# Layer 0 of a two-layer encoder: modulation steps from the last input piece on, short-conv taps beside the output projection, one more quarter in split products

## The chip, the cores and the metric

The kernel runs on one core of one Trainium2 chip. The metric is device time in microseconds (us) of the whole program; the time before is the median of three runs, 2281.75 us (2279.96 to 2282.76). Smaller is better.

## The reference

Two layers, each on 256 positions of 2048 channels in float32. Cut to what matters here (written with `*` for elementwise products):

```
mod = silu(c) @ w_mod[l] + b_mod[l]            # six vectors of 2048
shift_m, scale_m, gate_m, shift_f, scale_f, gate_f = split(mod)
h = layer_norm(x) * (1 + scale_m) + shift_m
proj = h @ w_in[l]                             # 2048 x 4288
uv, q_c, kv_c, k_r, sb, sc, sh, ag = split(proj)
y_a = gmlp(uv)                                 # group A: uses U and V columns
y_b = latent_attention(q_c, kv_c, k_r)         # group B
y_c = sb * causal_conv3(sc * sh)               # group C: E (=sb), C (=sc, sh)
y_d = silu(layer_norm(causal_conv31(a * sigmoid(g))))   # group D, a and g from ag
y = concat(y_a, y_b, y_c, y_d) @ w_out[l]      # 2048 x 2048
x = layer_norm(ALPHA * x + (1 + gate_m) * y)
h = layer_norm(x) * (1 + scale_f) + shift_f
y = (silu(causal_conv3(gate)) * val) @ ffn_w_down,  gate, val = split(h @ ffn_w_up)
x = layer_norm(ALPHA * x + (1 + gate_f) * y)
```

Only layer 0 from the end of its input projection to the end of its output projection is touched.

## The kernel before, in words

**Two kinds of product.** A weight is used either exactly (float32, tiles `wexact`, one DMA straight into place, PE takes two passes) or split: the DMA brings `wraw`, ACT rounds it to `whi` (L461), DVE subtracts to get `wlo` (L462), and PE does three products of the rounded kind in their place, `whi` with the rounded data, `wlo` with it, `whi` with the data's rest. The tiles of a raw load come from a pool of four 1 MB buffers (`rawp`), which modulation loads (`wmod`) share; the split and the exact tiles come from `splitp`, four of each of two tags (`weights`, L426). In the output projection `plain` lists the column chunks that use exact weights.

**Modulation.** For a vector of `mod`, DVE multiplies each 128x2048 block of w_mod by one column of silu(c) and adds it into `macc` (`mod_step`, L235 to L240), sixteen steps a vector; a bias row is added for gates (L358). `mod_stream` (L338) yields after each step, with the sums on PE (`ps_gate` for a gate, L289; `ps_mod` for the others) done as chores in between. The order of vectors is GATE_M, SHIFT_F, SCALE_F, GATE_F of layer 0, then layer 1's. `pump` (L376) adds the phase's rate from RATES to a credit and does as many steps as the credit holds; `stream` (L405) calls it once for each unit of work, and issues that unit's weight loads first.

**Order of layer 0.** `by_pieces` (L1299) takes the input's contraction rows in five PIECES as their modulation gets ready; in each piece PE does D's products and between them those of the groups U, V and E (`side`). Then follow group B (`latent_group`, eight units, exact), group C (1024 columns, eight units, exact), and the output projection (`out_proj`, L669) in the column chunks (0, 1024), (1024, 512), (1536, 512): eight units split, four exact, four exact, with a unit of a 512-wide chunk holding four contraction tiles and of the first chunk two. The last chunk's products are done at the end, first tile t = 0, then t = 1, with the norm's work on DVE.

**Background work.** `background` holds small jobs that `stream` takes, `bg` of them per unit; `drain_background` does the rest at once. STEPS gives `bg` by phase: the conformer conv's thirty taps on DVE (`convD`, L920), each with four scalings on ACT (L919) into `scaled`, and `norm_d`. `attend` (L1080) follows group B: it transposes the copied latent rows on PE into `ps_q`, `ps_kv`, and goes on to `kc`, `ps_kr`, `ps_qn`. `mix_c` and `conv_c` (L1247: one ACT scaling and two DVE taps for each of four blocks, `yc`) and `mix_e` (L1261: `yc` times E's sums) are done in one go after C. `out_proj`'s `load_unit` (L795) splits the data too (`act_pair`, `split`).

**Engines.** Each engine takes its instructions in the order in which the program is written down by this Python code, so what is pumped or drained where sets the order on DVE, ACT, PE and the DMA queue of SP. Tiles' buffers come free when their last reader is done.

Of the kernel before, what the change touches and what calls it, by code (L numbers as in the profile page):

```python
# [18 lines left out]
KT = D // P  # L19
# [13 lines left out]


RATES = [
    dict(B=1.6, C=2.2, out=1.5, up=0.7, down=0.7),
    dict(D=1.0, U=0.0, V=0.0, B=0.0, C=0.0, E=0.9, out=0.6, up=0.3, down=0.7),
]

STEPS = [  # L40
    dict(B=1, C=3, up=2),
    dict(U=7, B=4, C=4, E=8, up=2),
]

PIECES = ((0, 2), (2, 2), (4, 4), (8, 4), (12, 4))
# [5 lines left out]
def encoder_kernel(ctx: ExitStack, tc: tile.TileContext, A: dict, consts: bass.AP, out: bass.AP):  # L51
# [321 lines left out]
    def phase(l, name):  # L373
        pace["rate"] = RATES[l][name]
# [26 lines left out]
    def drain_background():  # L401
        while background:
            background.pop(0)()
# [214 lines left out]
    def run(g):  # L618
        units, load, products, end, bg = g
        for u in range(units):  # L620
            stream(lambda: load(u), lambda item, u=u: products(item, u), bg)
            pending.extend(postponed)
            postponed.clear()
        pending.append(end)
# [44 lines left out]
    def out_proj(l, w, src, order, gate_of, name, post_g, post_b, before, then, plain=(), bg=0):  # L669
# [113 lines left out]
        for c0, width in CHUNKS:  # L783
            last = c0 + width == D
            nk = 2048 // width
            units = nkt // nk
            state = {"tail": []}

            def load(u, c0=c0, width=width, nk=nk, units=units, last=last):
                item = load_unit(u, c0, width, nk, units, last)  # L790
                if last and u == units - 1:
                    gains()
                return item

            def load_unit(u, c0, width, nk, units, last):  # L795
                kt = order[nk * u]
                assert order[nk * u : nk * u + nk] == list(range(kt, kt + nk))
                spare = nk if last and units - 4 <= u < units - 2 else 0
                exact = c0 in plain
                parts = weights(w, kt, nk, c0, width, exact, spare)  # L800
                s4 = src[kt // 4]
                if exact:
                    return parts, [(s4[:, kt % 4 + k, :], None) for k in range(nk)]
                acts = []
                for k in range(0, nk, 2):
                    pair = kept.get(kt + k)
                    if pair is None:
                        pair = act_pair("a")
                        split(pair, s4[:, kt % 4 + k : kt % 4 + k + 2, :])
                        if nkt == KT:  # L810
                            kept[kt + k] = pair
                    for j in range(2):
                        acts.append([h[:, j, :] for h in pair[:2]])
                return parts, acts

            def unit(item, u, state=state, c0=c0, width=width, nk=nk, last=last, units=units):
                if u == 0:
                    state["ps"] = [
                        [acc_tile(f"{name}_{c0}{t}{i}") for i in range(width // 512)] for t in range(2)
                    ]  # L820
                if last and u >= units - 4:
                    state["tail"].append((item, u))
                    return
                for t in range(2):
                    products(t, item, state["ps"], u, nk)

            for u in range(units):
                stream(lambda: load(u), lambda item, u=u, unit=unit: unit(item, u), bg, not last)

            def done(state=state, c0=c0, nk=nk, last=last):  # L830
                if c0 == 0:
                    box["gate"] = gate_of()
                for t in range(2):
                    for item, u in state["tail"]:
                        products(t, item, state["ps"], u, nk)
                    if t == 0 and last and before is not None:
                        before()
                for t in range(2):
                    finish(t, state["ps"], c0)
                    if last:  # L840
                        norm(t)
                if last:
                    closed.append(True)

            pending.append(done)


    def mixers(l, w_in, Y, hF=None, between=None):
# [397 lines left out]

        def conv_c(ch):  # L1247
            yc = Y["c"] = slot("yc").rearrange("p (j s) -> p j s", j=4)
            for j in range(4):
                act.activation(out=yc[:, j, :], in_=ch[:, j, :], func=AF.Copy, scale=SW(2, j))  # L1250
                for k in range(2):
                    dve.scalar_tensor_tensor(
                        out=yc[:, j, 2 - k :],
                        in0=ch[:, j, : S - 2 + k],
                        scalar=SW(k, j),
                        in1=yc[:, j, 2 - k :],
                        op0=ALU.mult,
                        op1=ALU.add,
                    )

        def mix_e(cps, _):  # L1261
            yc = Y["c"]
# [36 lines left out]
    def by_pieces(l, w_in, hF, between, mix_d, mix_u, gelu_v, mix_v, mix_b, mix_c, mix_e):  # L1299
# [49 lines left out]
        for q, (k0, nkt) in enumerate(PIECES):  # L1349
            ahead = between(q + 1) if q + 1 < len(PIECES) else ([], None)  # L1350
            exact = k0 < PLAIN_KT
            loaded = {}

            def load(g, kt):

                c0, width = (C_AG, 1024) if g == "D" else (cols[g], 512)
                nk = min(2048 // width, nkt)
                for j, p in enumerate(weights(w_in, kt, nk, c0, width, exact or g != "D")):
                    loaded[(g, kt + j)] = p

            mods_left = list(ahead[0])
            units = len(mods_left)

            def some_mods(share):
                while mods_left and (units - len(mods_left)) < units * share:
                    mods_left.pop(0)()

            def d_part(kt, half):
                if ("D", kt) not in loaded:
                    load("D", kt)  # L1370
                chan_major(accD, kt, loaded[("D", kt)], range(4 * half, 4 * half + 4), kt == 0, kt == KT - 1)

            turns_d = [(kt, h) for kt in range(k0, k0 + nkt) for h in range(2)]
            n = len(turns_d) // 4
            for s in range(4):
                mine = turns_d[s * n : (s + 1) * n]
                if ("D", mine[0][0]) not in loaded:
                    load("D", mine[0][0])
                some_mods((0.3, 0.7, 1.0, 1.0)[s])
                if s == 3 and ahead[1] is not None:  # L1380
                    ahead[1]()
                for kt, h in mine:
                    d_part(kt, h)
                if s < 3:
                    g = "UVE"[s]
                    load(g, k0)
                    some_mods((0.5, 0.85, 1.0)[s])
                    side(g, [(kt, loaded[(g, kt)]) for kt in range(k0, k0 + nkt)], k0, nkt)
        mix_d(accD, None)
        mix_u(sums["U"], None)  # L1390
        for t in range(2):
# [5 lines left out]

        def mix_ce(cps, tps):
            mix_c(cps, tps)
            mix_e(sums["E"], None)  # L1400

        run(group(w_in, C_SC, 1024, f"C{l}", mix_ce, hF=hf, bg=STEPS[l]["C"]))
        drain_background()
# [151 lines left out]
    for l in range(DEPTH):  # L1555
        Y = {}
        if l == 0:
            hF = [slot(f"hF{q}").rearrange("p (j s) -> p j s", j=4) for q in range(4)]
            mixers(l, A["w_in"][l], Y, hF, lambda q: piece(q, hF))
        else:  # L1560
            mixers(l, A["w_in"][l], Y)
        phase(l, "out")
        flush()
        out_proj(
            l,
            A["w_out"][l],
            [Y[n] for n in "abcd"],
            list(range(KT)),
            gate(l, GATE_M),
            f"o{l}",  # L1570
            A["post_mix_g"][l],
            A["post_mix_b"][l],
            needs(l, SHIFT_F, SCALE_F),
            modulated(l, SHIFT_F, SCALE_F),
            plain=(1024, 1536) if l == 0 else (),
        )
        phase(l, "up")
        if l + 1 < DEPTH:
            turns.extend(load_params(l + 1))
        G = []  # L1580
        ffn_up(l, G)
        phase(l, "down")
        flush()
        out_proj(
            l,
            A["ffn_w_down"][l],
            G,
            list(range(NF)),
            gate(l, GATE_F),
            f"d{l}",  # L1590
            A["post_ffn_g"][l],
            A["post_ffn_b"][l],
            needs(l + 1, SHIFT_M, SCALE_M) if l + 1 < DEPTH else None,
            modulated(l + 1, SHIFT_M, SCALE_M) if l + 1 < DEPTH else None,
        )
# [63 lines left out]
```

## Time and profile before

| | |
|---|---|
| median of three runs | 2281.75 us (2279.96 to 2282.76) |
| the profiled execution | 2284.06 us, span 2282.3 us, mean PE clock 0.989 |
| group B's first to C's first product | 189.9 to 233.9 us |
| turn B to C and start of C's later products | 233.9 to 256 us |
| C's end, output projection's first product | 329.8, 330.5 us |
| end of first quarter pair, second chunk's first product | 388.5 us |
| modulation steps | 2.3 us each on DVE, 1 MB of DMA each |

The page tells busy time by engine, the chain that ended last, groups of instructions by line, and DMA issues. Engines: PE matmul, PEld weight load, DVE, ACT, POOL, SP. A view row of the timeline reads start, duration, engine, line, operation, written tile <- read tiles, shape, and in brackets the idle time before it and who ended it. A window row reads length, then busy time (and instructions) of each engine, the PE clock granted (1.00 is full), the share of the DMA engines and GB/s.

### The profile page before, as it was taken

The numbers are of one execution on the slowest core, as the hardware profiler recorded it, in microseconds if no ns is written. First come the engines' busy times: TensorE is split into PE (matmuls) and PEld (weight loads), VectorE is DVE, ScalarE is ACT, GpSimd is POOL, SyncE is SP. The second block draws the span as 40 slices with busy tenths as digits, with TensorE's granted clock in tenths as the row PEclk, the third lists the DMA queues.
The fourth block names the chain that finished last, engine by engine and source line by source line (L and its number), as shares of the span: only waits on it lengthen the run. The fifth ranks groups of instructions, "written<-read, shape, count | busy, mean of one in ns | idle before, by whom it ended". The sixth has DMA issues, their size and how long they took to land. (4 is left out here: it accounts for less than half of the span.)

```text
span 2282.3 us, 28994 instructions
## 1 busy us (share of the span) xinstructions
PE 2216.6 (97%) x11118; PEld 1823.0 (80%) x11118; DVE 1781.2 (78%) x2192; ACT 1111.3 (49%) x1693; POOL 37.2 (2%) x61
## 2 busy tenths in 40 slices
PE   5899999999999999999999999999999999999997
PEld 4686777478888888887886888877888888888886
DVE  6877889588899899898977997887776565565676
ACT  2234652264554554544556545556555454454553
POOL 2000000000000000000000000000000000000000
PEclk9999999999999999999999999999999999999999
DMA  9999879778888988888875755966665555555554
GB/s 348 368 336 337 334 261 379 282 263 327 309 326 300 333 312 327 318 318 295 323 269 195 236 186 175 328 247 226 240 224 183 195 182 194 190 196 187 197 190 147
DMA packets 228691, 604.11 MB, mean 265 GB/s; under 512 B 14580, under 2 KB 27108, under 8 KB 206788
## 3 DMA queue, kind: packets, MB, share of 16 engines
q1 hardware_dynamic: 227704, 601.25, 74.3%
q8 instruction: 87, 1.43, 0.2%
q0 software_dynamic: 848, 1.01, 0.1%
q14 instruction: 52, 0.43, 0.0%
HBM read 600.11 MB, written 2.10 MB: 264 GB/s over the span
## 5 line engine op out<-in xcount | busy, mean ns | idle before, releaser
L461 ACT CAST whi<-wraw 128x1024 fp32r<-128x1024 f32 (+1 forms) x624 | 649.7, 1048 | 705.6 <-PE g_c L79 198.6
L462 DVE TENSOR_TENSOR wlo<-wraw,whi 128x1024 fp32r<-128x1024 f32 (+1 forms) x624 | 749.0, 1214 | 309.0 <-ACT whi L461 301.8
L79 PE MATMUL v_c<-hT,whi 128*128 128x512 f32 x1408 | 491.4, 393 | 0.0
L79 PE MATMUL g_c<-hT,whi 128*128 128x512 f32 x1280 | 446.8, 393 | 0.0
L79 PE MATMUL v_c<-hT,wlo 128*128 128x256 f32 x1408 | 394.1, 280 | 0.0
L79 PE MATMUL d<-whi,a 128*128 128x512 f32 x1344 | 387.9, 390 | 0.0
L240 DVE SCALAR_TENSOR_TENSOR macc<-wmod,cact,macc 128x2048 f32<-128x2048 f32 x150 | 352.0, 2347 | 18.2 <-DMA wmod<-in_w_mod_dram 18.0
L79 PE MATMUL g_c<-hT,wlo 128*128 128x256 f32 x1280 | 358.2, 280 | 0.0
L79 PEld LDWEIGHTS v_c<-hT,whi 128*128 128x128 f32 x1408 | 263.6, 187 | 59.5
L79 PEld LDWEIGHTS d<-whi,a 128*128 128x128 f32 x1344 | 252.8, 188 | 52.6
L79 PEld LDWEIGHTS g_c<-hT,whi 128*128 128x128 f32 x1280 | 239.7, 187 | 54.3
L79 PEld LDWEIGHTS v_c<-hT,wlo 128*128 128x128 f32 x1408 | 265.8, 189 | 0.2
L79 PEld LDWEIGHTS g_c<-hT,wlo 128*128 128x128 f32 x1280 | 241.7, 189 | 0.2
L79 PE MATMUL d<-wlo,a 128*128 128x512 f32 x672 | 233.7, 390 | 1.9 <-DVE wlo L462 1.9
L79 PEld LDWEIGHTS d<-wlo,a 128*128 128x128 f32 x672 | 126.5, 188 | 29.0 <-DVE wlo L462 2.7
L79 PE MATMUL o<-whi,a 128*128 128x512 f32 x352 | 102.4, 398 | 0.0
L480 ACT CAST a<-g 128x512 fp32r<-128x512 f32 x132 | 81.3, 617 | 36.0 <-PE d L79 33.3
L481 DVE TENSOR_TENSOR a<-g,a 128x512 fp32r<-128x512 f32 x132 | 87.8, 685 | 1.8 <-ACT a L480 1.8
L605 PE MATMUL first<-wexact,hN 128*128 128x512 f32 x192 | 85.5, 595 | 1.2 <-ACT hN L82 0.8
L240 DVE SCALAR_TENSOR_TENSOR qacc<-wmod,cact,qacc 128x1024 f32<-128x1024 f32 (+1 forms) x75 | 80.2, 1070 | 2.4 <-DMA wmod<-in_w_mod_dram 0.4
L79 PEld LDWEIGHTS o<-whi,a 128*128 128x128 f32 x352 | 67.1, 192 | 15.3 <-ACT whi L461 1.0
L1448 DVE SCALAR_TENSOR_TENSOR u<-g,pf,u 128x254 f32<-128x254 f32 (+1 forms) x176 | 73.8, 479 | 0.4 <-ACT u L82 0.2
(355 smaller groups left out, 2497.6 us busy)
## 6 DMA issues: line engine op xcount, KB each, us to landing
wraw<-in_ffn_w_up_dram SPq DMA_DIRECT2D x168, 1024.0 KB, 5.2
wmod<-in_w_mod_dram SPq DMA_DIRECT2D x160, 1024.0 KB, 6.5
wraw<-in_ffn_w_down_dram SPq DMA_DIRECT2D x88, 1024.0 KB, 5.2
wmod<-in_w_mod_dram SPq DMA_DIRECT2D x64, 512.0 KB, 7.4
wraw<-in_w_in_dram SPq DMA_DIRECT2D x30, 1024.0 KB, 7.2
wexact<-in_w_in_dram SPq DMA_DIRECT2D x52, 512.0 KB, 7.6
wraw<-in_w_out_dram SPq DMA_DIRECT2D x24, 1024.0 KB, 6.5
wexact<-in_w_out_dram SPq DMA_DIRECT2D x16, 512.0 KB, 12.7
```

Of the source, the lines that this page charges most:

```text
L79: pe.matmul(o, lhsT, rhs, start=start, stop=stop, skip_group_check=True)
L240: i = dve.scalar_tensor_tensor(out=acc, in0=w, scalar=col, in1=acc, op0=ALU.mult, op1=ALU.add)
L461: held(act.copy(hi[:, :m], r), "cast")
L462: i = dve.tensor_tensor(out=lo[:, :m], in0=r, in1=hi[:, :m].bitcast(F32), op=ALU.subtract)
L480: act.copy(hi, src)
L481: dve.tensor_tensor(out=lo, in0=src, in1=hi.bitcast(F32), op=ALU.subtract)
L605: i = pe.matmul(ps, hN[kt // 4][:, kt % 4, t * P : (t + 1) * P], parts[kt], start=kt == 0, stop=kt == KT - 1, skip_group_check=True,)
L1448: dve.scalar_tensor_tensor(out=u[:, sh:], in0=x[:, : S - sh], scalar=col(k, j), in1=u[:, sh:], op0=ALU.mult, op1=ALU.add)
```

## The change

RATES, STEPS, the last piece's pumping and three pieces of code are changed. In the last piece of the input, three pumps at rate 2.0 take six GATE_M steps; B's rate falls from 1.6 to 1.5, C's rises from 2.2 to 2.4, the output projection's falls from 1.5 to 0.95. The conformer conv's taps go from one to two per unit in B, and from three per unit in C to none in the first two units and three in the other six. Short conv's four blocks and the product with E's sums become background jobs in layer 0, two per unit of the output projection, with a drain ahead of contraction tile 8. The chunk (1024, 512) leaves `plain`, so its weights are split.

```diff
 RATES = [
-    dict(B=1.6, C=2.2, out=1.5, up=0.7, down=0.7),
+    dict(last=2.0, B=1.5, C=2.4, out=0.95, up=0.7, down=0.7),
...
 STEPS = [
-    dict(B=1, C=3, up=2),
-    dict(U=7, B=4, C=4, E=8, up=2),
+    dict(B=2, C=(0, 0, 3, 3, 3, 3, 3, 3), out=2, up=2),
+    dict(U=7, B=4, C=4, E=8, out=0, up=2),
 ]
...
     def run(g):
         units, load, products, end, bg = g
         for u in range(units):
-            stream(lambda: load(u), lambda item, u=u: products(item, u), bg)
+            steps = bg if isinstance(bg, int) else bg[u]
+            stream(lambda: load(u), lambda item, u=u: products(item, u), steps)
...
             def load_unit(u, c0, width, nk, units, last):
                 kt = order[nk * u]
+                if nkt == KT and c0 == 0 and kt == KT // 2:
+                    drain_background()
...
         def conv_c(ch):
             yc = Y["c"] = slot("yc").rearrange("p (j s) -> p j s", j=4)
-            for j in range(4):
+
+            def block(j):
                 act.activation(out=yc[:, j, :], in_=ch[:, j, :], func=AF.Copy, scale=SW(2, j))
...
+            for j in range(4):
+                if hF is None:
+                    block(j)
+                else:
+                    background.append(lambda j=j: block(j))
...
+            if q == len(PIECES) - 1:
+                phase(l, "last")
             for s in range(4):
...
                     side(g, [(kt, loaded[(g, kt)]) for kt in range(k0, k0 + nkt)], k0, nkt)
+                    if q == len(PIECES) - 1:
+                        pump()
...
         def mix_ce(cps, tps):
             mix_c(cps, tps)
-            mix_e(sums["E"], None)
+            background.append(lambda: mix_e(sums["E"], None))
...
-            plain=(1024, 1536) if l == 0 else (),
+            plain=(1536,) if l == 0 else (),
+            bg=STEPS[l]["out"],
```

## The prediction

> **What bounds the kernel now.** First the page, for the engine that sets the end: its head and the row of busy times.
>
> ```profile
> span 2282.3 us, 28994 instructions
> PE 2216.6 (97%) x11118; PEld 1823.0 (80%) x11118; DVE 1781.2 (78%) x2192; ACT 1111.3 (49%) x1693; POOL 37.2 (2%) x61
> ```
>
> PE works 97% of the span, so the end moves only by PE's own work, by its idle time, or by its clock. Second, PE's waits from 150 to 481 us, the part of layer 0 that the change touches.
>
> ```profile
> PE o L79 <- DVE wlo L462: 4.9, 2, 4.7
> PE ps_mix L79 <- DVE va L1013: 2.2, 1, 2.2
> PE ps_q L1087 <- ACT qg L1093: 1.6, 1, 1.6
> ```
>
> Columns: total, times, longest. There are 8.7 us to win in these rows, nearly all in three places: the output projection's first chunk, the start of group B, the turn from B to C. Third, the windows of those stages (PE busy, PEld, DVE, ACT, POOL, PE clock, DMA share, GB/s).
>
> ```profile
> 190.00:234.00 44.00, 41.81 (x146) 27.54 (x146) 38.39 (x39) 26.14 (x61) 1.64 (x2) 0.96 0.95 339
> 234.00:258.00 24.00, 21.67 (x89) 17.07 (x88) 16.51 (x16) 17.22 (x48) 1.63 (x3) 0.86 0.78 311
> 330.00:345.00 15.00, 9.96 (x37) 7.26 (x38) 15.00 (x23) 8.35 (x16) 0.00 (x0) 0.94 0.63 212
> 345.00:389.00 44.00, 43.70 (x193) 34.66 (x192) 39.16 (x30) 11.53 (x12) 0.00 (x0) 0.94 0.98 374
> 389.00:417.00 28.00, 28.00 (x67) 12.46 (x66) 20.59 (x19) 0.00 (x0) 0.00 (x0) 1.00 1.03 403
> ```
>
> In group B (190 to 234) DVE has 5.6 us free and the DMA engines 5%; from 330 to 345 DVE has nothing free and PE loses 5 us. The neighbours of PE are full here, so work put on DVE earlier has to be paid for by something later.
>
> **Part 1: modulation from the last piece on, taps at 2 per unit in B.** The rates still give 48 steps by the end of the output projection: before 8x1.6+8x2.2+12x1.5=48; after 3x2+8x1.5+8x2.4+12x0.95=48.6. But GATE_M's sixteen steps now all stand before the end of B, and with them, in the compiled order of the changed kernel, GATE_M's first row sum (ps_gate) stands on PE directly behind B's last product, then one ps_q, and only then C's first sixteen products, which before stood directly behind B. So PE now waits at the turn for two things: DVE's last GATE_M step with its bias row, and ACT's copies of the latent rows.
>
> How late is DVE? These rows of before give every item.
>
> ```profile
> 190.79 1.28 DVE L864 TENSOR_TENSOR gluD<-D_c,sg 128x512 f32<-128x512 f32 x2
> 195.31 2.35 DVE L240 SCALAR_TENSOR_TENSOR macc<-wmod,cact,macc 128x2048 f32<-128x2048 f32 x1 [3.24 <-DMA wmod<-in_w_mod_dram]
> 197.58 0.68 DVE L1004 COPY wT<-ps_wT 64x512 f32<-64x512 f32 x1
> ...
> 201.58 1.41 DVE L1013 SCALAR_TENSOR_TENSOR va<-va,rs_A,gmlp 128x512 f32<-128x512 f32 x2
> ...
> 206.79 0.42 DVE L1026 TENSOR_TENSOR mixed<-ps_mix,gmlp 128x256 f32<-128x256 f32 x1
> ...
> 208.25 0.68 DVE L1032 TENSOR_TENSOR ya<-ya,mixed 128x512 f32<-128x512 f32 x1
> ...
> 209.98 2.35 DVE L240 SCALAR_TENSOR_TENSOR macc<-wmod,cact,macc 128x2048 f32<-128x2048 f32 x1
> 212.24 1.20 DVE L920 TENSOR_TENSOR convD<-convD,scaled 128x1008 f32<-128x1008 f32 x1
> 213.36 2.35 DVE L240 SCALAR_TENSOR_TENSOR macc<-wmod,cact,macc 128x2048 f32<-128x2048 f32 x1
> ```
>
> ```profile
> 260.70 2.27 DVE L358 TENSOR_TENSOR macc<-macc,brow 1x2048 f32<-1x2048 f32 x1
> ```
>
> A step and a tap take 213.36-209.98=3.38 us, of which the tap is 213.36-212.24=1.12. After gluD (ends 192.1) the changed DVE queue holds, ahead of the end of the bias row: wT to va, 202.99-197.58=5.4; four mixed and two ya, 4x0.34+2x0.6=2.6 (the durations less their overlap); ten steps and twelve taps, 10x3.38+2x1.12=36.0; the bias row 2.3. Sum 46.3: it ends at 238.4 at the earliest, if no step waits for its DMA. PE gets there at 231.3 (233.9 in before, less the 2.2 us wait for va and a little of its low clock). That is 7 us of idle PE.
>
> Then ps_q. ACT's queue has, ahead of the copies that ps_q reads, the scaling for tap 239, whose buffer comes free with DVE's tap 241: three taps behind the bias row, 238.4+3.4=241.8. The rest of ACT's chain is sized by before:
>
> ```profile
> 232.37 0.48 ACT L1062 ACTIVATE junk<-B_w 128x384 f32<-128x384 f32 x1
> ...
> 235.94 0.31 ACT L1070 COPY lat<-B_w 128x128 f32<-128x128 f32 x1
> ```
>
> From 232.37 to 236.25 is 3.9 us, of which some 0.7 stand ahead of the stall, so 3.2 are left and ps_q starts near 245. PE then begins C's products 13.7 us after B's last one, with 0.9 us of ps_gate in between. The rows of the turn in before:
>
> ```profile
> 233.89 7.07 PE L79 MATMUL C_c<-hF,wexact 128*128 128x256 f32 x32
> 240.80 0.60 PE L1087 MATMUL ps_q<-cst,lat 128*128 128x128 f32 x4
> 242.97 0.77 PE L1087 MATMUL ps_q<-cst,lat 128*128 128x128 f32 x4 [1.57 <-ACT qg L1093]
> ```
>
> and two windows of low clock, behind ps_q and behind the wait at 342:
>
> ```profile
> 246.00:250.00 4.00, 3.78 (x10) 2.34 (x9) 3.88 (x4) 1.23 (x3) 0.00 (x0) 0.50 0.39 98
> 342.00:346.00 4.00, 3.35 (x9) 2.66 (x10) 4.00 (x4) 2.69 (x5) 0.00 (x0) 0.65 1.02 330
> ```
>
> C's products start 11 us later than at 233.89. Against that the waits behind ps_q (1.6 and less) partly go, since C's products now cover them, and in exchange PE runs cold: the window from 246 to 250 has a clock of 0.50 after waits of that size, and now C's sixteen run cold instead. I take both together as -0.8 and the term of part 1 as **+10.2 us** at C's end. Bounds: +6 if the tap chain on ACT costs nothing beyond DVE's 7 us, +13 if a GATE_M step also waits for its wmod as one did in before for 3.2 us. C itself has no wait of PE to win.
>
> The Trainium skill ("TensorE: Matmul & The Clock Gate", Architectural detail) says that PE pulls only weight loads ahead, matmuls stay in program order, and ACT and DVE are strict queues. No row of before can show it here. If instead C's sixteen products could be taken ahead, 6.9 us of the stall would be filled; that is a rival below.
>
> The last piece costs nothing: its wmods now stand in front of the wraw of its last two kt, whose products PE needs some 2 us after the split by the pitches above. Bounds 0 to +2.
>
> **Part 2: short conv's taps and mix_e beside the output projection.** Before, they stood between C and the splits:
>
> ```profile
> 336.39 1.52 PE L79 MATMUL o<-whi,a 128*128 128x512 f32 x6
> 337.02 3.24 DVE L1252 SCALAR_TENSOR_TENSOR yc<-chC,pm,yc 128x254 f32<-128x254 f32 x8
> 341.38 2.36 DVE L462 TENSOR_TENSOR wlo<-wraw,whi 128x1024 fp32r<-128x1024 f32 x2
> 342.65 0.79 PE L79 MATMUL o<-wlo,a 128*128 128x512 f32 x2 [4.74 <-DVE wlo L462]
> ```
>
> DVE did the taps (3.24), the product with sumE (1.2) and then the split, and PE waited 4.74. In the new order each of units 0 and 1 has one step, four taps of 0.4 and two splits: 2.26+1.6+2.36=6.2 us of DVE against PE's unit. A PE unit of a split chunk is 24 products; the chain that ended last gives the pitch:
>
> ```profile
> 2031.01 239.70 PE d L79 x1056
> ```
>
> 239.70/1056=0.227 us, a unit is 5.45. So DVE is 0.8 us late in a unit of that kind, 0.65, 1.3 and 0.35 in the next three: 3.1 in place of 4.9. The gain is small, and it goes if ACT's or DMA's share is late.
>
> **Part 3: third quarter split, fewer steps in the output projection.**
>
> ```profile
> 388.47 7.11 PE L79 MATMUL o<-wexact,ya 128*128 128x512 f32 x16
> 395.41 7.03 PE L79 MATMUL o<-wexact,yb 128*128 128x512 f32 x16
> ```
>
> An exact unit takes 395.41-388.47=6.94, four 27.6. Split it is 96 products, 96x0.227=21.8: -5.8. It adds eight casts on ACT, which has room (0.00 busy from 389 to 417), and eight splits on DVE at 1.21, by the page's row:
>
> ```profile
> L462 DVE TENSOR_TENSOR wlo<-wraw,whi 128x1024 fp32r<-128x1024 f32 (+1 forms) x624 | 749.0, 1214 | 309.0 <-ACT whi L461 301.8
> ```
>
> DVE's split of the second of these units now stands behind the first quarter's norm work, which an exact chunk hid:
>
> ```profile
> 386.79 1.28 DVE L701 TENSOR_TENSOR yg<-o,gate 128x512 f32<-128x512 f32 x2
> 387.99 2.34 DVE L240 SCALAR_TENSOR_TENSOR macc<-wmod,cact,macc 128x2048 f32<-128x2048 f32 x1
> 390.25 1.29 DVE L702 SCALAR_TENSOR_TENSOR x<-x,yg 128x512 f32<-128x512 f32 x2
> 391.45 1.28 DVE L705 BATCH_NORM_STATS2 st_o<-x 128x6 f32<-128x512 f32 x2
> ```
>
> Between the two pairs of splits stand nine of these at 0.6 and a step, 7.7 us, and the pair itself 2.36: 10.0 against one unit of 5.45, so PE waits about 4.5, and 0.3 for the unit before. After such an idle time PE ran cold for about 4 us (clock 0.65 from 342 to 346): at half speed +2.0. The wait needs no rate; it can only shrink if DVE comes into the chunk early (0) or grow with a late wraw (+3).
>
> Whole stretch from C's end to the fourth quarter, before: 330.46 to 388.47+27.6=416.1, 85.6 us. After: SHIFT_F's column sum, which now comes between C and o,
>
> ```profile
> 355.50 3.63 PE L79 MATMUL ps_mod<-ones,macc 128*128 128x1 f32 x32
> ```
>
> 3.6, eight units 43.6, four 21.8, waits 3.1 and 4.8, cold 2.0: 78.9. Parts 2 and 3 together **-6.7 us**; without any wait of PE it would be 69, -16.6 us; with each wait doubled, +3.
>
> The fourth quarter and the norm are unchanged. At the start of `up`, DVE's copies, a step and four u now stand before the split of unit 1, by an estimate from such rows (0.6 to 0.7 a copy, 2.26 a step, less than 0.5 an u) 5 us of DVE under 4 of PE's products ahead: **+1.0** (0 to +4). Behind it both kernels have the same steps at the same rate.
>
> **The sum.** +10.2-6.7+1.0=+4.5 on the profiled execution's 2284.06 (span 2282.3 and 1.8 around it) is 2288.6. That execution was 2.3 above the median of the three runs, 2281.75, so the forecast is 2281.75+4.5, about **2286.3 us**.
>
> The skill's same page (What's actually happening) says that the clock falls after an idle window of 3.4 us. The trace differs: it fell to 0.50 after the 1.57 us wait behind ps_q. By the page, the 3.1 us of short waits of part 2 cost no clock; the sum has none for them either.
>
> **The rivals.**
>
> A, the other side, faster: the turn from B to C doesn't stall. Mechanism: DVE reaches the bias row as PE reaches ps_gate, because more taps or steps than counted lie before gluD. It decides when the bias row ends before 231 us and ACT's scaling of tap 239 isn't ahead of PE. For it: DVE waited 3.2 us for a DMA before 195.31, so it has slack if the wmods land sooner. Against it: the 46.3 us are summed from durations. Then part 1 is worth the 2.2 us wait and 1.7 of clock, -3.9: -3.9-6.7+1.0=-9.6, 2272.2.
>
> B, slower: the stall in full and the output projection gains nothing, because DVE's late split in the second quarter and one late wraw (the four raw buffers are all the pool has, and the DMA share is 0.98) eat 5.8 and 0.9 us. +10.2+0+1.0=+11.2, 2293.
>
> C, a wash: half of the stall is filled, by 6.9 us of C's products or as much of DVE's work gone: 2286.3-6.9=2279.4.
>
> That the change doesn't do what it says is excluded: the compiled order has the split products, the taps and the steps where the diff puts them.
>
> **How the numbers follow.** Forecast 0.45, its own range 2282.5 to 2290; A 0.22; B 0.23; C 0.10. A difference under 0.2% (4.6 us, about what a measurement of this kernel can tell from no change) is none: 2277.2 to 2286.3. The forecast lies on its upper edge, so half of its chance is within: same 0.22+0.10=0.32; slower 0.23+0.23=0.46; faster 0.22. The range runs from 2272 (half of A outside) to 2296 (a tenth of the rest outside).
>
> **What would show it.** In the changed profile: a PE wait of 5 us or more before ps_gate or ps_q near 231 us, put down to DVE L358 or ACT's latent copies, and C's end near 340. In the output projection PE's waits for wlo: none of 4.7 us in the first chunk, one of 3 to 5 early in the second quarter, which itself is 22 to 29 us long. No wait of that size at 231 means A; one in the first chunk of 5 us again means B.

## The result and the profile after

The changed kernel takes 2287.44 us, median of ten runs (2283.56 to 2289.27); the kernel before takes 2281.12 over its ten (2276.28 to 2283.79). The ratio is 1.0026, 95% interval 1.0018 to 1.0035: about 6 us slower (4 to 8 by the interval). Its profiled execution took 2287.58 us, only 3.5 us more than that of before, so the single executions below do not hold the whole difference. First the page of the changed kernel: PE still has 97%, and DVE has a little more to do.

```profile
span 2285.8 us, 29102 instructions
PE 2213.5 (97%) x11150; PEld 1830.2 (80%) x11150; DVE 1789.6 (78%) x2200; ACT 1117.6 (49%) x1701; POOL 36.5 (2%) x61
```

PE's waits of the changed kernel from 150 to 490 us (total, times, longest):

```profile
PE ps_gate L79 <- DVE macc L358: 5.9, 1, 5.9
PE ps_q L1090 <- ACT lat L1072: 4.8, 1, 4.8
PE o L79 <- DVE wlo L462: 4.3, 2, 4.1
PE B_w L79 <- DMA wexact<-in_w_in_dram: 1.6, 2, 1.3
```

The 4.7 us before the output projection's wlo and the 2.2 us for va are gone; two waits of together 10.7 us have come at the turn from B to C, and one of 4.1 us into the third quarter. The turn on PE:

```profile
234.27 0.70 PE L79 MATMUL B_n<-wexact,hF 128*128 128x320 f32 x2
240.87 2.04 PE L79 MATMUL ps_gate<-macc,ones 128*128 128x512 f32 x2 [5.90 <-DVE macc L358]
247.76 0.48 PE L1090 MATMUL ps_q<-cst,lat 128*128 128x128 f32 x1 [4.84 <-ACT lat L1072]
248.03 9.50 PE L79 MATMUL C_c<-hF,wexact 128*128 128x256 f32 x32
```

C's sixteen products (two records each) take 9.50 us here and 7.07 before: PE is cold after the waits (clock 0.74 from 248.0 to 257.4; before, 1.00 from 233.9 to 240.8). DVE and ACT at that place show what PE waits for:

```profile
238.45 2.27 DVE L358 TENSOR_TENSOR macc<-macc,brow 1x2048 f32<-1x2048 f32 x1
240.65 2.42 DVE L923 TENSOR_TENSOR convD<-convD,scaled 128x972 f32<-128x972 f32 x2
```

```profile
241.84 3.20 ACT L922 ACTIVATE scaled<-gluD,pm 128x241 f32<-128x241 f32 x8 [1.61 <-DVE convD L923]
...
245.44 0.48 ACT L922 ACTIVATE scaled<-gluD,pm 128x239 f32<-128x239 f32 x1
...
247.35 0.35 ACT L1072 COPY lat<-B_w 128x256 f32<-128x256 f32 x1
```

The bias row ends at 240.7. DVE then goes on with taps, ACT's scalings wait for them until 241.8 and end at 245.0, ACT's own chain of copies follows, and the copy for ps_q is ready at 247.7. Last the output projection:

```profile
341.86 3.86 PE L79 MATMUL ps_mod<-ones,macc 128*128 128x1 f32 x32
346.19 1.22 PE L79 MATMUL o<-whi,a 128*128 128x512 f32 x2 [0.47 <-ACT whi L461]
393.54 0.51 PE L79 MATMUL o<-wlo,a 128*128 128x512 f32 x1 [0.17 <-DVE wlo L462]
403.45 0.80 PE L79 MATMUL o<-wlo,a 128*128 128x512 f32 x1 [4.13 <-DVE wlo L462]
420.89 3.59 PE L79 MATMUL o<-wexact,ya 128*128 128x512 f32 x8
```

From these marks and those of before, the difference by stage in the two profiled executions:

| stage on PE | before | after | difference |
|---|---|---|---|
| start to B's first product | 189.9 | 193.0 | +3.1 |
| B's first to C's first product | 44.0 | 55.1 | +11.1 |
| C's first product to C's end | 96.6 | 93.8 | -2.8 |
| C's end to the fourth quarter | 85.6 | 79.0 | -6.6 |
| fourth quarter to the first transpose | 32.7 | 34.4 | +1.7 |
| first transpose to L0's first product d | 506.3 | 507.0 | +0.6 |
| first d to layer 1's first product | 278.0 | 274.3 | -3.7 |
| the rest | 1049.2 | 1049.3 | +0.1 |

C's end is the start of whatever stands behind C on PE: o before, SHIFT_F's column sum (ps_mod) after. The fourth quarter's mark of before is 416.1, the third quarter's start and four units of 6.9 us, since six of the fourth quarter's records stand among the third's at 402.28.

One profiled execution tells a stage to about 1 to 2 us, as runs with the same code in a stage show. B's first product stands between 189.7 and 190.8 us in nine of the ten experiments that have the six steps in the last piece, but at 192.3 in the tenth, e13, and at 192.2 in e4, which has none: the +3.1 is an execution's own scatter for the larger part. From C's end to the fourth quarter e3 and e10 take 78.9 and 80.3 us with the code of the changed kernel (79.0), and from there to the first transpose both take 32.7, like before, where the changed kernel took 34.4.

### The profile page after: what moved, and what is told of

It is laid out like the page before. It is cut to its first block, busy times and chain, and to the rows that moved or that the text cites. A ratio compares the mean times of both kernels' runs of the same rounds, so it can differ in the third digit from the quotient of the medians.

```text
span 2285.8 us, 29102 instructions
## 1 busy us (share of the span) xinstructions
PE 2213.5 (97%) x11150; PEld 1830.2 (80%) x11150; DVE 1789.6 (78%) x2200; ACT 1117.6 (49%) x1701; POOL 36.5 (2%) x61
## 5 line engine op out<-in xcount | busy, mean ns | idle before, releaser
L461 ACT CAST whi<-wraw 128x1024 fp32r<-128x1024 f32 (+1 forms) x632 | 656.9, 1045 | 738.5 <-PE g_c L79 200.4
L240 DVE SCALAR_TENSOR_TENSOR macc<-wmod,cact,macc 128x2048 f32<-128x2048 f32 x150 | 351.7, 2345 | 17.4 <-DMA wmod<-in_w_mod_dram 17.2
L79 PEld LDWEIGHTS v_c<-hT,whi 128*128 128x128 f32 x1408 | 263.8, 187 | 60.7
L79 PEld LDWEIGHTS g_c<-hT,whi 128*128 128x128 f32 x1280 | 239.9, 187 | 55.5
L79 PE MATMUL o<-whi,a 128*128 128x512 f32 x416 | 121.7, 397 | 0.5 <-ACT whi L461 0.5
L79 PEld LDWEIGHTS o<-whi,a 128*128 128x128 f32 x416 | 79.9, 192 | 17.4 <-ACT whi L461 0.6
L240 DVE SCALAR_TENSOR_TENSOR qacc<-wmod,cact,qacc 128x1024 f32<-128x1024 f32 (+1 forms) x75 | 80.2, 1070 | 2.4 <-DMA wmod<-in_w_mod_dram 0.4
L79 PE MATMUL o<-wlo,a 128*128 128x512 f32 x208 | 72.6, 400 | 4.3 <-DVE wlo L462 4.3
```

Of the source, the lines that this page charges most:

```text
L79: pe.matmul(o, lhsT, rhs, start=start, stop=stop, skip_group_check=True)
L240: i = dve.scalar_tensor_tensor(out=acc, in0=w, scalar=col, in1=acc, op0=ALU.mult, op1=ALU.add)
L461: held(act.copy(hi[:, :m], r), "cast")
```

## The experiments

Stage numbers are counted from B's first product in each run's own profiled execution. "C starts" is C's first product, "o" the output projection's first product, "xT" the first transpose behind it. Before o stands SHIFT_F's column sum (3.6 to 4.4 us) in all runs but before, e1, e12 and e13.

| run | C starts | o | xT | median us | ratio to before, interval |
|---|---|---|---|---|---|
| before | 44.0 | 140.5 | 258.8 | 2281.1 | |
| changed | 55.1 | 153.2 | 262.3 | 2287.4 | 1.0026, 1.0018 to 1.0035 |
| e1 | 40.9 | 137.6 | 257.1 | 2284.4 | 1.0009, 0.9999 to 1.0019 |
| e2 | 55.1 | 153.8 | 263.7 | 2289.1 | 1.0033, 1.0020 to 1.0045 |
| e3 | 50.3 | 157.1 | 264.4 | 2291.1 | 1.0043, 1.0027 to 1.0058 |
| e4 | 44.2 | 155.3 | 267.9 | 2295.5 | 1.0056, 1.0037 to 1.0074 |
| e5 | 55.0 | 153.8 | 260.3 | 2285.9 | 1.0015, 1.0001 to 1.0029 |
| e7 | 39.7 | 151.2 | 259.8 | 2282.5 | 0.9998, 0.9983 to 1.0013 |
| e8 | 39.7 | 150.7 | 260.2 | 2283.6 | 1.0006, 0.9991 to 1.0021 |
| e9 | 39.7 | 152.9 | 262.9 | 2284.2 | 1.0009, 0.9993 to 1.0025 |
| e10 | 55.5 | 155.1 | 263.8 | 2287.2 | 1.0030, 1.0018 to 1.0042 |
| e11 | 39.7 | 144.3 | 261.6 | 2290.6 | 1.0043, 1.0030 to 1.0056 |
| e12 | 39.7 | 143.9 | 261.0 | 2289.7 | 1.0037, 1.0025 to 1.0049 |
| e13 | 55.1 | 153.8 | 257.7 | 2282.3 | 1.0003, 0.9994 to 1.0012 |

**e1, the spread taps and the split quarter alone**, without the fewer steps that the prediction's part 3 names in its heading.

```diff
-    dict(last=2.0, B=1.5, C=2.4, out=0.95, up=0.7, down=0.7),
+    dict(last=0.0, B=1.6, C=2.2, out=1.5, up=0.7, down=0.7),
...
-    dict(B=2, C=(0, 0, 3, 3, 3, 3, 3, 3), out=2, up=2),
+    dict(B=1, C=3, out=2, up=2),
```

> Parts 2 and 3 without part 1: rates and taps as before (B=1.6, C=2.2, out=1.5, no steps in the last piece, one tap a unit in B, three in C), short conv's taps in the background of the output projection, third quarter split. Own theory (the loss sits at the turn from B to C, the gain in the output projection): no PE wait for the bias row and C's first product near 234 us; the stretch from C's end to the fourth quarter falls from 85.6 by 3 to 7 us, less than in the changed kernel since 18 steps instead of 11 lie in it; total 2275 to 2279. Rival one (the steps taken out of the output projection are what frees it, the split products give nothing): the stretch stays within 2 us of 85.6, total 2279 to 2284. Rival two (the stretch behind C costs later what it gains): stretch short, total unchanged.

PE's waits from C's end to the first transpose in this run:

```profile
PE o L79 <- DVE wlo L462: 9.1, 8, 2.5
PE o L79 <- ACT whi L461: 3.1, 3, 1.4
```

C's end to the fourth quarter takes 414.5-327.8=86.7 us where before took 85.6: the split quarter and the spread taps win nothing while eighteen steps lie in the stretch. Rival one is right on the stretch; the median, 2284.4, lies just above its range.

**e2, part 1 alone** (rates, steps of the last piece and taps as changed):

```diff
-                if hF is None:
-                    block(j)
-                else:
-                    background.append(lambda j=j: block(j))
+                block(j)
...
-            background.append(lambda: mix_e(sums["E"], None))
+            mix_e(sums["E"], None)
...
-            plain=(1536,) if l == 0 else (),
+            plain=(1024, 1536) if l == 0 else (),
```

> Part 1 alone: the changed rates, the last piece's steps and the changed taps, with short conv done at once after C and the third quarter exact as before. Own theory: PE waits 5 to 6 us for the bias row and 4 to 5 us for ACT's latent copies at the turn, C ends 8 to 10 us late, the output projection wins back 0 to 3 us by having 7 steps fewer: total 2286 to 2291. Rival (the turn costs little in the end, because C regains it, and the changed kernel loses elsewhere): total within 2 us of the kernel before.

It takes 2289.1 us, as its own theory had it. The waits at the turn are those of the changed kernel. What was not foreseen stands in the output projection:

```profile
339.62 3.63 PE L79 MATMUL ps_mod<-ones,macc 128*128 128x1 f32 x32
...
419.47 3.60 PE L79 MATMUL o<-wexact,ya 128*128 128x512 f32 x8
```

419.5-339.6=79.9 us from C's end to the fourth quarter, with short conv done at once and an exact quarter, against 79.0 in the changed kernel. So 5.7 of the 6.6 us that this stretch won come with part 1 alone, and the 0.9 that the other two parts would bring is within the scatter. By their records (L238 and L240) DVE does 17 steps in this stretch before and 12 in e2 and in the changed kernel. The rates promised seven fewer (18 against 11.4), but DVE still works off earlier ones here. PE's idle time in the stretch falls from 5.2 us before to 1.2 in e2; the rest of the 5.7 is PE's own time. e2 does not separate the fewer steps from the column sum's new place at C's end: there PE has 3.6 us to do while DVE and ACT get to the splits, and in e13, without that sum, PE waits 4.2 us for whi at this place.

**e5, the third quarter exact again.**

```diff
-            plain=(1536,) if l == 0 else (),
+            plain=(1024, 1536) if l == 0 else (),
```

> The changed kernel with the third quarter exact again, all else as changed. First theory (the split products are worth 5.8 us of PE, less 4.1 of wait and 2 of cold clock in their second unit): the wait of 4.1 us goes, the quarter takes 27.6 us without a wait, total within 2 us of the changed kernel, 2285.5 to 2289.5. Rival (the split is a clear gain, hidden by the turn): 3 to 6 us slower, 2290 to 2293. Rival (its eight splits on DVE cost more than they save): 3 us or more faster, under 2284.5.

2285.9 us, 1.6 under the changed kernel with intervals that overlap. The 4.1 us wait is gone, 0.3 us of wait for wlo is left. From C's end to the fourth quarter it takes 78.1 us where the changed kernel took 79.0:

```profile
339.81 3.63 PE L79 MATMUL ps_mod<-ones,macc 128*128 128x1 f32 x32
...
417.86 3.60 PE L79 MATMUL o<-wexact,ya 128*128 128x512 f32 x8
```

The first theory holds: the split saves no more than its second unit loses.

**e3, the taps as before.**

```diff
-    dict(B=2, C=(0, 0, 3, 3, 3, 3, 3, 3), out=2, up=2),
+    dict(B=1, C=3, out=2, up=2),
```

> The changed kernel with STEPS of B and C as before (one tap a unit in B, three in every unit of C). In its order ps_gate still stands right behind B's last product, but C's first sixteen products stand ahead of ps_q. Own theory (two waits in a row, DVE's bias row and then ACT's taps ahead of the copies): the wait for the bias row stays at 4 to 7 us, the wait before ps_q of 4.8 us goes, total 3 to 6 us under the changed kernel, 2281 to 2284. Rival (only the bias row matters, PE waits for it as long as for both): total that of the changed kernel, 2286 to 2288.

2291.1 us: both forecasts missed. C's products do come before ps_q, but PE waits all the same:

```profile
239.18 2.05 PE L79 MATMUL ps_gate<-macc,ones 128*128 128x512 f32 x2 [7.18 <-DVE macc L358]
241.02 7.73 PE L79 MATMUL C_c<-hF,wexact 128*128 128x256 f32 x32
248.59 0.60 PE L1090 MATMUL ps_q<-cst,lat 128*128 128x128 f32 x4
255.12 1.11 PE L1090 MATMUL ps_q<-cst,lat 128*128 128x128 f32 x4 [5.93 <-ACT qg L1096]
```

```profile
249.25 5.46 ACT L922 ACTIVATE scaled<-gluD,pm 128x239 f32<-128x239 f32 x14
```

```profile
250.53 1.15 DVE L923 TENSOR_TENSOR convD<-convD,scaled 128x956 f32<-128x956 f32 x1 [3.35 <-ACT scaled L922]
```

The second wait has moved from the copies to qg, which in ACT's queue stands behind fourteen scalings. ACT is the late engine both times, but here not for want of DVE: DVE itself waits 3.35 us for the scalings.

**e10, only the row sum later.**

```diff
-                if 1 <= kt < KT - 1:
+                if (4 if (l, m) == (0, SHIFT_F) else 1) <= kt < KT - 1:
                     chore()
```

> The changed kernel, only with the first four row-sum jobs starting at the fifth step of the next vector in place of the second, so that ps_gate stands inside C; steps, taps and rates as changed. In its order the first ps_q now stand directly behind B's last product. Own theory (the bias row and ACT's copies wait behind the same DVE queue, one inside the other): one wait of 9 to 11 us before ps_q in place of 5.9 and 4.8, C no earlier, total that of the changed kernel within 2 us. Rival (ps_gate is what holds C up): the wait shrinks to 5 us or less, total 4 to 7 us under the changed kernel.

```profile
244.54 0.96 PE L1090 MATMUL ps_q<-cst,lat 128*128 128x128 f32 x2 [13.23 <-ACT lat L1072]
245.29 9.84 PE L79 MATMUL C_c<-hF,wexact 128*128 128x256 f32 x32
```

One wait of 13.2 us (a little more than expected) and 2287.2 us: ps_gate held nothing up that ACT's copies would not have held up by themselves.

**e4, no steps in the last piece.**

```diff
-    dict(last=2.0, B=1.5, C=2.4, out=0.95, up=0.7, down=0.7),
+    dict(last=0.0, B=1.5, C=3.15, out=0.95, up=0.7, down=0.7),
```

> The changed kernel without steps in the last piece (rate 0 there), C takes them (3.15 for 2.4), all else as changed. The first row sum then stands inside C. Own theory: no wait of PE at the turn but those of before (2 us for va, 1.6 for qg), C's end within 2 us of before, the output projection 6 to 7 us shorter than before: total 2274 to 2278. Rival (the two taps a unit in B hold ACT's copies back also without the row sum): a wait of 3 to 5 us before ps_q stays, total 2278 to 2283. Rival (C cannot hold 25 steps): C's end moves out by 3 us or more.

C starts at 44.2, with no wait for the bias row, though inside its first sixteen products PE waits 2.0 us for a copy on ACT. The kernel is the slowest of all, 2295.5 us. Its largest waits:

```profile
PE o L79 <- DVE wlo L462: 9.3, 3, 5.0
PE ps_pT L1205 <- DVE p L1196: 2.8, 2, 2.0
PE ps_mix L79 <- DVE va L1016: 2.5, 1, 2.5
```

The last rival is right, and by far: C's end lies 151.8 us behind B's first product (before: 140.5), so C does not hold 25 steps, and then the output projection is late too. Whether the six steps could stand elsewhere than in the last piece, this run does not tell.

**e7, e8, e9: the row sum in C by other rates.** All three have the first diff; e7 has the third quarter exact, e9 (split like e8) the taps as before.

```diff
-    dict(last=2.0, B=1.5, C=2.4, out=0.95, up=0.7, down=0.7),
+    dict(last=2.0, B=1.1, C=2.6, out=1.05, up=0.7, down=0.7),
```

> The changed kernel with rates last=2.0, B=1.1, C=2.6, out=1.05, so that 15 instead of 18 steps are done by B's end and the first row sum stands inside C; third quarter exact. Own theory (DVE's row sum ahead of C on PE and the taps ahead of the copies on ACT are the loss; the fewer steps in the output projection are the gain): no wait of 5 us at the turn, C's end 2 to 4 us later than before counted from B's start, output projection as in the run with steps and taps only (109.9 us from its first product to the first transpose): total 2275 to 2280. Rival (DVE is full from B to the output projection, so what leaves the turn comes back as waits in C or later): total 2284 to 2290.

> As the run before (rates last=2.0, B=1.1, C=2.6, out=1.05), with the third quarter split. In its order the splits of the second unit stand ahead of the first quarter's norm work, so the 4.1 us wait should go too. Own theory: 2 to 5 us under the run with the third quarter exact, 2271 to 2277. Rival (DVE is full): no faster than with the exact quarter, waits for wlo elsewhere in the output projection of 4 us or more in sum.

> As the run before, with the taps as in the kernel before (one a unit in B, three a unit in C). It tells whether the taps' place matters once the row sum is out of the way. Own theory (taps ahead of ACT's copies matter only while DVE is late at the turn): within 3 us of the run before. Rival (two taps a unit in B are themselves the loss): 3 us or more faster than it; rival (the taps put into C hold C up): 3 us or more slower.

In all three C starts at 39.7, 15 us earlier than in the changed kernel, but the output projection starts only 2.0 us earlier (151.2 for 153.2). e7's waits in C, and windows of it:

```profile
PE ps_qr L79 <- DVE qc L1132: 2.8, 2, 1.9
PE ps_var L79 <- ACT sqD L945: 1.8, 2, 1.5
PE ps_q L1090 <- ACT qg L1096: 1.6, 1, 1.6
```

```profile
240.70:251.00 10.30, 9.72 (x31) 7.36 (x32) 8.60 (x7) 7.54 (x20) 0.00 (x0) 0.67 0.25 86
...
258.50:263.30 4.80, 4.80 (x17) 3.99 (x16) 4.68 (x7) 3.11 (x8) 0.00 (x0) 0.71 1.02 423
...
321.40:330.90 9.50, 7.71 (x31) 6.03 (x31) 3.25 (x8) 2.54 (x3) 0.70 (x1) 0.75 0.79 303
```

Some 7 us of short waits, and three stretches with or just behind them at 0.67 to 0.75 of the clock (the last but two numbers of a row). e7's median is that of the kernel before: it misses the 2275 to 2280 of its own theory, whose C's end came 6.4 us later than before and not 2 to 4, and it misses the rival's 2284 to 2290 too. e8's split quarter brings nothing once more, as the rival said (3.6 us of waits for wlo where it had named 4 or more), and e9 lies within 1 us of e8, as expected.

**e11, no steps in C's first two units** (on e7, so C=3.4 for six):

```diff
-            stream(lambda: load(u), lambda item, u=u: products(item, u), steps)
+            stream(lambda: load(u), lambda item, u=u: products(item, u), steps, isinstance(bg, int) or u >= 2)
```

> The run with the row sum later and the third quarter exact, with no modulation step in C's first two units (C=3.4 for the other six). There C's stretch took 107 us with a third of the waits of the turn: waits of 0.6 to 1.9 us for qc, kvr, qg and sqD, and a low clock behind them. Own theory (these short waits on DVE's queue and the cold clock behind each of them are what C loses): the two waits for qc (2.8 us) go, PE stays warm there, C 3 to 7 us shorter, total 2275 to 2279. Rival (DVE's work in sum is the limit, so it comes back as waits for sqD or wlo): total within 2 us of that run, 2280 to 2284.

The waits for qc go, and C's first product to ps_mod takes 97.4 us in place of 107.3. But then:

```profile
327.48 4.28 PE L79 MATMUL ps_mod<-ones,macc 128*128 128x1 f32 x32
334.64 1.65 PE L79 MATMUL o<-whi,a 128*128 128x512 f32 x3 [2.88 <-ACT whi L461]
339.98 1.22 PE L79 MATMUL o<-wlo,a 128*128 128x512 f32 x2 [3.69 <-DVE wlo L462]
```

SCALE_F's column sum waits another 3.9 us for its last step on DVE. o to xT takes 117.3 us for 108.6 in e7, and the total is 2290.6. The rival is right that DVE's work comes back later, and it even undershot the price.

**e13 and e12, the column sums.** In the changed kernel (e13) and in e11 (e12) SHIFT_F and SCALE_F are summed as layer 1's vectors are:

```diff
-        elif l > 0:
+        elif l > 0 or m in (SHIFT_F, SCALE_F):
             chores.extend(fold_cols(l, m, acc))
```

> The changed kernel, with only the two column sums on DVE. The same theory on the changed kernel: waits at the turn as in it, total 2280 to 2285 if DVE has the room in the output projection, 2287 to 2291 if not.

> As the run before, with SHIFT_F's and SCALE_F's column sums done as layer 1 does them, by transposes and reductions on DVE and four products on PE in place of sixteen products of one column. Theory (the clock falls behind the 3.6 us of one-column products though PE never pauses there, and the next products cost 1.5 to 2.5 us more): both stretches of low clock and 2 x 3.4 us of PE go, some 4 us of DVE for each vector come: total 3 to 8 us under the run before if DVE has the room, 0 to 4 over it if not.

e13 takes 2282.3 us, 5 us under the changed kernel and within 0.1% of the kernel before. The windows of the changed kernel just before ps_mod, in it, and behind it, and then those of e13 (PE clock is the last but two):

```profile
431.20:434.60 3.40, 3.40 (x9) 1.51 (x8) 0.37 (x3) 0.89 (x4) 0.00 (x0) 1.00 1.01 369
434.60:438.90 4.30, 4.30 (x34) 4.28 (x32) 0.69 (x1) 0.00 (x0) 0.00 (x0) 0.81 0.04 12
438.90:445.00 6.10, 6.10 (x10) 2.55 (x11) 5.83 (x14) 1.63 (x4) 0.99 (x1) 0.57 0.17 38
```

```profile
431.00:434.40 3.40, 3.40 (x9) 1.52 (x8) 0.16 (x1) 1.19 (x4) 0.00 (x0) 1.00 0.97 355
434.40:439.70 5.30, 5.30 (x26) 3.33 (x25) 3.50 (x9) 0.00 (x0) 0.00 (x0) 1.00 0.26 66
```

PE has no gap in any of them. The gain lies in this one place: from the fourth quarter to xT e13 takes 29.2 us, the changed kernel 34.4 (e3 and e10: 32.7). About half of it is the sum itself (in e13 both vectors' sums stand here, 0.8 us each, for 4.3 of SCALE_F's alone) and half the eight products behind. At C's end, where SHIFT_F's sum stood, nothing is won: PE waits 4.2 us for whi there instead. e12 missed its two ranges by falling between them: 0.9 us under e11, since there DVE, full as it is, lets PE wait 7.4 us for the reduced sums.

## Why the prediction was right, and where by luck

**The turn, part 1: right in mechanism and nearly in size.** The bias row was to end at 238.4 or later and ended at 240.7, the first ps_q was to start near 245 and started at 247.8; counted from B's first product, which was 3.1 us later in this execution, both are within 1 us. C's first product came 11.1 us late where 11 were forecast. The rest of the term was too pessimistic: C's stretch regained 2.8 us, not 0.8. Of these, 1.0 us is work that now stands ahead of C, two records of ps_gate and one ps_q; the forecast had counted them into the later start and not taken them out of C. Another 1.2 us is idle time (2.5 us in C's stretch before, 1.4 after), and some 0.6 is left for the clock: C's first products ran colder, ps_kr and ps_qn warmer (together 9.1 us before, 6.6 after). So the term is +8.3 in place of +10.2. e10 shows that ACT's copies behind the taps are enough to hold C up.

**The output projection: the sum right, its reasons mostly wrong.** -6.6 measured, -6.7 forecast, and the wait of 4.13 us in the second unit was forecast as 4.5. But its terms do not carry that sum. The first chunk's waits (3.1 for 4.9) give -1.8 and the split quarter with its wait and its cold clock (-5.8+4.8+2.0) gives +1.0. The other -5.9 has no reason in the text: the stretch of before holds 85.6-3.6-43.6-27.6-4.9=5.9 us beyond the items that the sum counts, and the sum for the changed kernel prices the same eight units without it. "Fewer steps" stands in part 3's heading and has no term of its own. The runs put the gain there: e1 has the spread taps and the split quarter and wins nothing, e2 has neither and wins 5.7 us. The split quarter is worth nothing by e5 (78.1 us with it exact, 79.0 split), as its own terms said. And two misses in the sum cancel: the first chunk waited 0.5 us and not 3.1, while PE was busy for 74.2 us of the stretch where the sum had 71.0.

**The start of `up`:** +0.6 up to L0's first d, forecast +1.0. That is not a test: in the experiments this stretch takes 503.9 to 509.6 us.

**The last piece** was to cost nothing, and in nine of the ten experiments with its six steps B's first product stands within 1 us of before's.

**What the sum left out.** The 1.7 us of the fourth quarter are scatter (32.7 us in e3 and e10). From the first d to layer 1 it is 3.7 us shorter: before has there

```profile
1083.66 0.62 PE L79 MATMUL d<-wlo,a 128*128 128x512 f32 x1 [1.91 <-DVE wlo L462]
```

which the changed kernel hasn't. Experiments with this wait (1.0 to 1.9 us in e1, e2, e5, e7 and others) take 275.5 to 276.4 us for the stretch, those without it 274.2 to 274.7. So 1.6 of the 3.7 us are before's own execution (278.0, where e1 and e2 take 276.4 with a wait of about the same length); why the wait comes and goes with steps that lie 700 us earlier stays open.

**The total** is right in part by luck: the three terms that were forecast measured +2.3 (8.3-6.6+0.6) and not +4.5, the two profiled executions differ by 3.5, and the medians by 6.3. Which stage holds the rest of the median's difference stays open. That the loss comes with part 1 is shown by e2 (1.0020 to 1.0045) against e1 (0.9999 to 1.0019). Two slips in the working change nothing: 8x1.6+8x2.2+12x1.5 is 48.4, and four units of 6.94 are 27.8 us.

**Rival A** (no stall at the turn) has been made to happen in e7, and it did not bring its -9.6: the time at the turn was taken back in C. **Rival B**'s form, no gain in the output projection, is what e1 shows when the steps stay there. **Rival C** asked what filling half of the stall is worth. C's products did not fill it: they stand behind both waits in the changed kernel. e7 has no such stall and gains 5 us on the changed kernel, with an exact third quarter.

A common cause is likely, but not shown: from B to the output projection DVE has 48 steps, 30 taps and the splits to do, and PE waits wherever too much of it stands ahead of what PE needs. In the changed kernel the stretches read (PE busy, PEld, DVE, ACT, POOL, clock, DMA share):

```profile
193.00:248.00 55.00, 42.62 (x149) 26.48 (x148) 54.03 (x49) 34.94 (x87) 1.64 (x2) 0.92 0.92 340
248.00:341.90 93.90, 92.54 (x430) 77.25 (x429) 72.65 (x83) 44.07 (x108) 2.33 (x4) 0.97 0.79 307
341.90:393.00 51.10, 50.59 (x227) 41.71 (x225) 47.71 (x47) 23.43 (x30) 0.00 (x0) 0.93 0.92 334
```

DVE is busy 54.0 of 55 us up to C, but has 21 us free in C; 8.1 of these, from 324.8 to 332.9, are one wait for PE's ps_mean, with steps behind it in DVE's queue:

```profile
332.88 1.42 DVE L940 SCALAR_TENSOR_TENSOR convD<-ps_mean,convD 128x256 f32<-128x256 f32 x4 [8.06 <-PE ps_mean L79]
334.22 2.34 DVE L240 SCALAR_TENSOR_TENSOR macc<-wmod,cact,macc 128x2048 f32<-128x2048 f32 x1
```

So it is not DVE's sum alone that binds, but also what stands where in its queue. e4, e7, e11 each moved steps away from the place that waited, and each time waits came back elsewhere. No run moved norm_d's part of that queue. No version beat the kernel before clear of noise; e13 with an exact third quarter (e5) was not tried.

## What to carry to other kernels

Before crediting a stretch's gain to the edit that lies in it, count what else has left it: run the edit alone (e1) and the rest alone (e2). When a measured stretch is compared with a computed one, compute both, or what the sum doesn't count turns up as a gain. Where a second engine is nearly full in a stage, moving its work may only move the wait; look at its free time stage by stage, and at what blocks its queue there. In a queue of fixed order, look at what stands ahead of a copy that PE needs, not only at what PE itself names as last.

## What the runs showed of the hardware that was not expected

PE's clock falls behind a run of one-column products, though PE shows no gap. In the changed kernel the 32 records of ps_mod fill 4.30 of 4.30 us, the clock there is 0.81, and 0.57 in the 6.1 us behind; with each column sum as four products between others (e13) it stays at 1.00, and the kernel gains 5 us in the median, about half of it by the shorter sums themselves. Behind before's first ps_mod the clock falls too, to 0.71 and 0.67:

```profile
355.50:359.00 3.50, 3.50 (x34) 3.50 (x32) 3.50 (x3) 0.00 (x0) 0.00 (x0) 1.00 1.00 397
359.00:362.00 3.00, 3.00 (x12) 2.42 (x12) 2.57 (x4) 1.17 (x2) 0.00 (x0) 0.71 0.93 328
362.00:364.50 2.50, 2.50 (x9) 2.01 (x8) 2.50 (x3) 0.83 (x1) 0.00 (x0) 0.67 0.95 315
```

The Trainium skill ("TensorE: Matmul & The Clock Gate", What's actually happening) ties the fall to an idle window of 3.4 us; here, 3.5 us of one-column products had the same effect without a gap in PE's records. Whether the single column or the length of the run of such products does it, no run separates. And two waits of together 10.7 us cost about 2.4 us of clock (C's first sixteen products, 9.50 for 7.07), while e7's short waits, 7 us in sum, left three stretches of 5 to 10 us each at 0.67 to 0.75. Short waits do not always do so: in the changed kernel PE was busy for 3.24 of the 4.60 us from 257.4 to 262.0, and the clock there and up to 270 is 1.00.
